# A hybrid RWKV-7 / GLA layer on one core: the second direction's heads in exchanged halves of the array, weight products two groups at a time, and eight tiles moved to a later stage

## The chip, the core and the metric

The kernel is one program on 1 core of a Trainium2 chip. The metric is the device time of one launch in microseconds (us): the median of 3 runs was 1365.04 us (1364.23 to 1368.11).

Engines are named as the profile names them: PE (TensorE, PEld are its weight loads), DVE (VectorE), ACT (ScalarE), POOL (GpSimd) and SP, which issues the DMAs.

## The reference, cut to what matters

256 context tokens and 256 latent tokens of width 2048 go through one layer. A modulated RMSNorm gives `h`; one wide product gives the columns of everything else:

```python
p = h @ lp["w_in"]
(rkv, z_a, lora_w, lora_a, q_b, k_b, v_b, z_b, lora_g, g_a, g_b) = jnp.split(p, _split_points(), axis=-1)
```

An RWKV-7 branch (16 heads of 64) and a GLA branch (4 heads) scan the tokens in both directions, context first; only the latent tokens give output:

```python
y_a = (y_a + bonus.reshape(bsz, t, A_WIDTH)) * jax.nn.silu(f["z_a"])
ob = o_b * lax.rsqrt(jnp.mean(o_b * o_b, axis=-1, keepdims=True) + EPS) * lp["b_norm_g"]
y_b = ob.reshape(bsz, t, B_WIDTH) * jax.nn.silu(f["z_b"])
mixed = (jax.nn.sigmoid(f["g_a"]) * (y_a.astype(dt) @ lp["w_a"])
         + jax.nn.sigmoid(f["g_b"]) * (y_b.astype(dt) @ lp["w_b"]))
return mixed @ lp["w_out"]
```

A gated residual and a last RMSNorm follow. RWKV's per-head step is `S <- S diag(w) + (S a) b^T + v k^T`, `y = S r`.

## The kernel before

**Weight products.** Every weight tile (512 KB) is loaded from HBM as `raw`, split in ACT and DVE into a high part `wH` (a copy) and a low part `wL` (the rest), and multiplied in three matmuls: high by high, low by high, high by low. Such a group of three is the unit in which the order below speaks; on the page it is `acc<-lH,wH`, `acc<-lL,wH`, `acc<-lH,wL` (latent tokens alone, 256 columns) or `acc<-hH,...` (both streams, 512 columns); `pv` and `pout` are the same in other shapes. One tile of 128 columns of `w_in` takes 16 groups. A queue of jobs (`add_cm` and others) says in which order the tiles come; a job can carry a condition (`take`) and be passed over while that fails (`skip`).

**Who sets the order.** The code does not write instructions down in program order. Each piece of work is a generator (a track: `gla_track`, `sc_track`, `inv_track`, ...) that yields operations, bank claims or conditions. `Issue.run` keeps its own clocks of the five engines, built on a table of costs, and emits, step by step, the track that can start first; tracks that start within 40 ns of each other go by priority, and weight products have the last priority, 99: they fill where nothing else is ready. Two rules let a weight product go ahead of ready work: when 1.2 us of other work has gone since the last one (`since`), and when PE's clock threatens to fall by the table (`cooling`). What is emitted is a fixed order for each engine: if an operand is late on the chip, PE stands still, whatever is ready behind.

**The stages.** (1) Modulation vectors, RMSNorm and the first products (0 to 130 us of the profile). (2) The GLA stage, 130 to 582 us: the four GLA heads, the key and value tiles of RWKV (convolved, spilled to DRAM), and, two for each head, the eight tiles of `z_b` (`add_zb`, `sz_track` with key `"b"`): a tanh on ACT, a product on DVE, and the tile waits in SBUF until `gla_track` multiplies it with the transposed head (`pT`) and writes it to `yb` in DRAM. (3) The RWKV stage, 582 to 1166 us, for eight pairs of heads, `p` = 0 to 7. Its filler are the weight products of `r` and `z_a` (as slots come free) and of 32 tiles of the gates, `tg`; `pace` lets tile n go when n <= 17 + 32 x (small work done / 230 us), and all of them after the last pair's features (`"C"`). (4) The products with `w_b`, `w_a` (1166 to 1257 us) and `w_out` (to the end).

**A pair in stage 3.** `fe_track` makes features. `ab_track` makes eight chunk matrices for two directions `d` and two heads `hd`: fp32 matmuls 64 by 64 by 64 (`pab`), which read the half `hd` of the rows and write the half `hd` of the columns. `AB` is their masked copy. `inv_track` inverts them: ACT copies into `Lin`, a DVE transpose to `M`, 60 POOL operations (`tm`, `M`), transposes back, the products `pH` and `pZ`, and copies to `Z`. `sc_track` then goes through eight chunks, a chain in which each step needs the one before: `p1` (matmuls, `p` on the page), a copy `R` on ACT, `pU` (matmuls with `Z`), copies to `UV` on ACT and DVE, `pSs` (matmuls), `Sn` on DVE, copies to `UV`, and in the last four chunks products for the output, `pY`. Names for halves are `half(hd)`: partitions 0 to 63 or 64 to 127. An fp32 matmul stands twice in the profile (two passes): four matmuls are x8 there.

Of the kernel before, what the change touches and what calls it, by code (L numbers as in the profile page):

```python
# [76 lines left out]
class Issue:  # L77
# [253 lines left out]
def hybrid_layer(tc, a, out):  # L331
    nc = tc.nc
    es = ExitStack()
    with es:
# [197 lines left out]
        PACE0, WB = 17, 230e3  # L532
# [213 lines left out]
        yb = dp.tile([P, 8, 256], F32, name="yb")  # L746
        kv = [[dp.tile([P, 512], F32, name=f"kv{i}_{j}") for j in range(2)] for i in range(8)]
# [42 lines left out]

        def sz_track(acc, key):

            if key[0] == "b":
                yield S_sz.has()
                S_sz.n -= 1
# [43 lines left out]
        def gla_track(h, gp):  # L839
# [106 lines left out]
            for j in range(2):  # L946
                yield lambda: ("b", 2 * h + j) in szs
                pT = yield Claim("gg", [P, 2, P], "pT", *ons)
                yield [PE.transpose(pT[:, tt, :], ons[tt][:, j * P:j * P + P], ident) for tt in range(2)]
                sz = szs.pop(("b", 2 * h + j))  # L950
                yield DV.scalar_tensor_tensor(sz, pT.rearrange("p a b -> p (a b)"), bnh[:, j:j + 1], sz,
                                              op0=OP.mult, op1=OP.mult)
                rel(pT)
                yield DM.dma_start(yb[:, 2 * h + j, :], sz)
# [213 lines left out]
        def inv_track(p, fp, xp):  # L1168
# [11 lines left out]
            for hd in range(2):  # L1180
                for blk in range(2):
                    r = slice(64 * hd + 32 * blk, 64 * hd + 32 * blk + 32)
                    cc = slice(32 * blk, 32 * blk + 32)
                    yield AC.copy(RW["Lin"][qs[hd]].rearrange("p t u -> p u t")[:, 16 * blk:16 * blk + 16, :],
                                  AB[r, :, :, cc].rearrange("p i d t -> p (i d) t"))
            yield DV.transpose(M.rearrange("p i c -> p (i c)"), Lin.rearrange("p t u -> p (t u)"))
            for hd in range(2):
                yield AC.copy(RW["GMo"][qs[hd]], AB[64 * hd:64 * hd + 32, :, :, 32:64].rearrange("p i d t -> p (i d) t"))
# [21 lines left out]
            pZ = yield Claim("g3", [P, 16, 32], "pZ", GMo, Lin)  # L1210
            for u in range(0, 16, hq):
                yield [PE.matmul(pZ[64 * hd:64 * hd + 32, u + x, :], RW["GMo"][qs[hd], u + x, :], W[qs[hd], 16 + u + x, :],
                                 start=True, stop=True, tile_position=(qs[hd].start, 64 * hd)) for x in range(hq) for hd in range(2)]
            yield lambda: p < 2 or ("sc1", p - 2) in DONE
            for hd in range(2):
                for blk in range(2):
                    r = slice(64 * hd + 32 * blk, 64 * hd + 32 * blk + 32)
                    yield (DV.tensor_copy if hd else AC.copy)(Z[r, :, 32 * blk:32 * blk + 32], W[qs[hd], 16 * blk:16 * blk + 16, :])
                yield (DV.tensor_copy if hd else AC.copy)(Z[64 * hd:64 * hd + 32, :, 32:64], pZ[64 * hd:64 * hd + 32])
            rel(pZ)  # L1220
# [35 lines left out]
        def sc_track(p, xp):  # L1256
# [8 lines left out]
            for i in range(8):  # L1265
# [6 lines left out]
                b = [PE.matmul(p1[half(hd), d, :], GM[kr, hd, i, d, :], UV[kr, i, d, hd, :], start=True, stop=True)  # L1272
# [187 lines left out]
        def add_zb(i):  # L1460
            add_cm(w_in, C_ZB + P * i, "l", CTX, 12, lambda acc: sz_track(acc, ("b", i)))

# [50 lines left out]
        def pace(n):  # L1513
            return lambda: "C" in DONE or n <= PACE0 + 32 * (iss.small - state.get("b0", iss.small)) / WB

        for n in range(32):
            add_cm(w_in, (C_GA, C_GB)[n % 2] + P * (n // 2), "l", CTX, 12, lambda acc, n=n: tg_track(acc, n // 2, n % 2),
                   take=pace(n), skip=True)
# [132 lines left out]
        state["b0"] = iss.small  # L1651
        iss.groups["acc"] = (0, 1)
# [159 lines left out]
```

## Time and profile before

| what | value |
|---|---|
| median of 3 runs | 1365.04 us |
| the profiled execution's own time | 1361.36 us |
| its span, first to last instruction | 1359.6 us |
| mean granted clock of TensorE | 0.977 |
| busy share of the span: PE, DVE, ACT, POOL | 93%, 71%, 53%, 40% |
| PE matmuls in the trace | 11479 |

Matmuls are pipelined, and the profile models their ends, so a busy PE is not one at its peak. What one kind of work costs PE is read from the distance between starts in the timeline, not from the durations. The granted clock is 1.00 at 2.4 GHz and 0.50 at 1.2 GHz; a mean between them is a mix.

### The profile page before, as it was taken

The numbers are of one execution on the slowest core, as the hardware profiler recorded it, in microseconds if no ns is written. First come the engines' busy times: TensorE is split into PE (matmuls) and PEld (weight loads), VectorE is DVE, ScalarE is ACT, GpSimd is POOL, SyncE is SP. The second block draws the span as 40 slices with busy tenths as digits, with TensorE's granted clock in tenths as the row PEclk, the third lists the DMA queues.
The fourth block names the chain that finished last, engine by engine and source line by source line (L and its number), as shares of the span: only waits on it lengthen the run. The fifth ranks groups of instructions, "written<-read, shape, count | busy, mean of one in ns | idle before, by whom it ended". The sixth has DMA issues, their size and how long they took to land. (4 is left out here: it accounts for less than half of the span.)

```text
span 1359.6 us, 29662 instructions
## 1 busy us (share of the span) xinstructions
PE 1270.1 (93%) x11479; PEld 1068.1 (79%) x11479; DVE 968.3 (71%) x2031; ACT 718.2 (53%) x1449; POOL 543.3 (40%) x684
## 2 busy tenths in 40 slices
PE   5999999999999999999899999799989999999996
PEld 3555578688788897998777778677878888999876
DVE  4433497885965737767978998698978776668656
ACT  5222244343334444486577678667766666445443
POOL 0000476676570000005888729673983550000012
PEclk9999999999999999999889999799979999999999
DMA  9999465455462433576632443234433545789564
GB/s 347 354 340 311 132 195 168 150 171 160 145 202 79 134 102 97 153 196 171 157 85 76 113 118 92 77 99 114 108 78 94 138 105 145 203 247 271 185 230 144
DMA packets 311186, 220.45 MB, mean 162 GB/s; under 512 B 37354, under 2 KB 286724, under 8 KB 310532
## 3 DMA queue, kind: packets, MB, share of 16 engines
q1 hardware_dynamic: 311044, 218.55, 55.5%
q8 instruction: 90, 1.47, 0.4%
q14 instruction: 52, 0.43, 0.1%
HBM read 199.76 MB, written 12.46 MB: 156 GB/s over the span
## 5 line engine op out<-in xcount | busy, mean ns | idle before, releaser
L304 DVE TENSOR_TENSOR wL<-raw,wH 128x512 fp32r<-128x512 f32 x484 | 377.2, 786 | 170.2 <-ACT wH L304 165.0
L304 ACT CAST wH<-raw 128x512 fp32r<-128x512 f32 x484 | 295.1, 616 | 328.5 <-PE acc L304 208.7
L304 PE MATMUL acc<-lH,wH 128*128 128x256 f32 x896 | 285.1, 318 | 0.5 <-ACT tg L304 0.5
L304 PE MATMUL acc<-lL,wH 128*128 128x256 f32 x896 | 256.0, 286 | 0.0
L304 PE MATMUL acc<-lH,wL 128*128 128x256 f32 x896 | 255.6, 285 | 0.2 <-DVE wL L304 0.2
L304 PEld LDWEIGHTS acc<-lH,wH 128*128 128x128 f32 x896 | 173.4, 194 | 21.1 <-issue 4.5
L304 POOL TENSOR_TENSOR tm<-M 64x30 f32<-64x30 f32 (+14 forms) x240 | 160.1, 667 | 74.3 <-DVE M L304 48.1
L304 POOL TENSOR_TENSOR M<-M,tm 64x30 f32<-64x30 f32 (+14 forms) x240 | 170.1, 709 | 18.7
L304 PEld LDWEIGHTS acc<-lL,wH 128*128 128x128 f32 x896 | 174.5, 195 | 3.1 <-issue 1.7
L304 PEld LDWEIGHTS acc<-lH,wL 128*128 128x128 f32 x896 | 173.9, 194 | 0.4 <-DVE wL L304 0.4
L304 PE MATMUL acc<-hH,wH 128*128 128x512 f32 (+1 forms) x416 | 168.7, 406 | 1.3 <-ACT lo L304 1.3
L304 PE MATMUL acc<-hH,wL 128*128 128x512 f32 (+1 forms) x416 | 157.2, 378 | 0.0
L304 PE MATMUL acc<-hL,wH 128*128 128x512 f32 (+1 forms) x416 | 156.3, 376 | 0.1
L304 PEld LDWEIGHTS acc<-hH,wH 128*128 128x128 f32 x416 | 78.6, 189 | 38.1 <-issue 22.9
L304 POOL TENSOR_TENSOR xs<-yg,fg 128x512 f32<-128x512 f32 (+1 forms) x10 | 13.5, 1371 | 231.4 <-DVE yg L304 231.4
L304 POOL TENSOR_TENSOR gw<-gw,csl 128x512 f32<-128x512 f32 x60 | 71.1, 1185 | 61.9 <-DMA gw<-in_w_mod_dram 61.9
L304 PEld LDWEIGHTS acc<-hH,wL 128*128 128x128 f32 x416 | 78.4, 188 | 15.5 <-DVE wL L304 0.4
L304 POOL TENSOR_TENSOR ga<-ga,gw 128x512 f32<-128x512 f32 x60 | 88.6, 1476 | 4.2
L304 PEld LDWEIGHTS acc<-hL,wH 128*128 128x128 f32 x416 | 78.9, 190 | 10.6 <-DVE hL L304 0.4
L304 PE MATMUL acc<-yH,wH 128*128 128x256 f32 x256 | 73.0, 285 | 0.0
L304 PE MATMUL acc<-yL,wH 128*128 128x256 f32 x256 | 72.8, 284 | 0.0
L304 PE MATMUL acc<-yH,wL 128*128 128x256 f32 x256 | 72.8, 284 | 0.0
(318 smaller groups left out, 2627.7 us busy)
## 6 DMA issues: line engine op xcount, KB each, us to landing
raw<-in_w_in_dram SPq DMA_DIRECT2D x174, 512.0 KB, 4.0
wm<-in_w_mod_dram SPq DMA_DIRECT2D x64, 512.0 KB, 6.9
gw<-in_w_mod_dram SPq DMA_DIRECT2D x64, 256.0 KB, 4.0
raw<-in_w_out_dram SPq DMA_DIRECT2D x32, 512.0 KB, 4.8
raw<-in_w_b_dram SPq DMA_DIRECT2D x16, 512.0 KB, 4.1
raw<-in_w_a_dram SPq DMA_DIRECT2D x16, 512.0 KB, 4.9
kv<-kvo SPq DMA_DIRECT2D x16, 256.0 KB, 3.9
tg<-tg SPq DMA_DIRECT2D x32, 128.0 KB, 3.8
```

Of the source, the lines that this page charges most:

```text
L304: op = Op("dma" if name == "dma_start" else self.key, name, lambda: f(*a, **k), aps[0], aps[1:], func, k.get("accum_out"), any(x.tensor.na ...
```

## The change

It has four parts. (a) In `ab_track`, `inv_track` and `sc_track` the second direction's heads (`d` = 1) go to exchanged halves, `half(hd ^ d)`, and the results of the two directions to banks of their own: the four matmuls of `pab` and of `pU` use all four pairs of row half and column half, where before two of them used the same pair. The copies around them are cut by direction: two copies to `UV` after `pU` become four of half the size, four into `Lin` eight, and so for `GMo` and `Z`. (b) `Issue.run` counts the weight products since the last other PE work (`dense`); in stage 3, while that is under 500 ns by its table, the next group follows if it can start within 60 ns, though other work is ready. (c) The eight `z_b` tiles leave stage 2 and become the first of the paced filler jobs of stage 3 (`zs_track`: as before, but spilled to DRAM); `gla_track` only scales its head (on ACT), and `y_track` loads the tiles back and multiplies. (d) The pace is 25 + 40 x (small work done / 230 us), the 32 gate tiles counted from 8.

```diff
+        self.dense = self.run_min = 0.0
...
+                if tr[6] == "pe" and best[0] != 99 and 0 < self.dense < self.run_min:
+                    best = next((x for w, x in c if x[0] == 99 and isinstance(x[3], list)
+                                 and w <= max(w0, self.t["pe"]) + 60), best)
                 if tr[6] == "pe" and best[0] != 99 and 0.6 and self.cooling():
...
                 if best[0] == 99:
                     self.since = 0.0
+                    self.dense += self.work - w0
                 else:
+                    if best[6] == "pe":
+                        self.dense = 0.0
...
-        PACE0, WB = 17, 230e3
+        PACE0, NPACE, WB = 25, 40, 230e3
...
+        zs = [dp.tile([P, 256], F32, name=f"zs{i}") for i in range(8)]
...
+        def zs_track(acc, i):
+
+            yield S_tg.has()
+            S_tg.n -= 1
+            sz = pools["com"].tile([P, 256], F32, name="zs", tag="tg", bufs=2)
+            yield AC.activation(sz, acc, AF.Tanh, scale=0.5)
+            yield DV.scalar_tensor_tensor(sz, sz, 1.0, acc, op0=OP.add, op1=OP.mult)
+            rel(acc)
+            yield DM.dma_start(zs[i], sz)
+            S_tg.n += 1
+            DONE.add(("zs", i))
...
-                yield lambda: ("b", 2 * h + j) in szs
+                yield S_sz.has()
+                S_sz.n -= 1
...
-                sz = szs.pop(("b", 2 * h + j))
-                yield DV.scalar_tensor_tensor(sz, pT.rearrange("p a b -> p (a b)"), bnh[:, j:j + 1], sz,
-                                              op0=OP.mult, op1=OP.mult)
+                ob = pools["com"].tile([P, 256], F32, name="ob", tag="sz", bufs=2)
+                yield AC.activation(ob, pT.rearrange("p a b -> p (a b)"), AF.Copy, scale=bnh[:, j:j + 1])
...
+            pas = []
+            for d in range(2):
+                pas.append((yield Claim("g3", [P, 8, 64], f"pab{d}", *bks, ar)))
             for g in range(2):
-                pa = yield Claim("g3", [P, 4, 2, 64], "pab", *bks, ar)
-                yield [PE.matmul(pa[half(hd), i, d, :], bks[d][half(hd), chunk(4 * g + i, d), xb, :], ar[half(hd), d, i, g, :],
-                                 start=True, stop=True) for i in range(4) for d in range(2) for hd in range(2)]
-                yield DV.tensor_tensor(AB[:, 4 * g:4 * g + 4], pa, RW["m_t"][:, None, None, :].to_broadcast([P, 4, 2, 64]), op=OP.mult)
-                rel(pa)
+                yield [PE.matmul(pas[d][half(hd ^ d), 4 * g + i, :], bks[d][half(hd), chunk(4 * g + i, d), xb, :],
+                                 ar[half(hd), d, i, g, :], start=True, stop=True)
+                       for i in range(4) for d in range(2) for hd in range(2)]
+            for d in range(2):
+                yield DV.tensor_tensor(AB[:, :, d, :], pas[d], RW["m_t"][:, None, :].to_broadcast([P, 8, 64]), op=OP.mult)
+                rel(pas[d])
...
-                for blk in range(2):
-                    r = slice(64 * hd + 32 * blk, 64 * hd + 32 * blk + 32)
-                    cc = slice(32 * blk, 32 * blk + 32)
-                    yield AC.copy(RW["Lin"][qs[hd]].rearrange("p t u -> p u t")[:, 16 * blk:16 * blk + 16, :],
-                                  AB[r, :, :, cc].rearrange("p i d t -> p (i d) t"))
+                for d in range(2):
+                    for blk in range(2):
+                        r = slice(64 * (hd ^ d) + 32 * blk, 64 * (hd ^ d) + 32 * blk + 32)
+                        cc = slice(32 * blk, 32 * blk + 32)
+                        yield AC.copy(RW["Lin"][qs[hd]].rearrange("p t u -> p u t")[:, 16 * blk + 8 * d:16 * blk + 8 * d + 8, :],
+                                      AB[r, :, d, cc])
...
-                b = [PE.matmul(p1[half(hd), d, :], GM[kr, hd, i, d, :], UV[kr, i, d, hd, :], start=True, stop=True)
+                b = [PE.matmul(p1[half(hd ^ d), d, :], GM[kr, hd, i, d, :], UV[kr, i, d, hd, :], start=True, stop=True)
...
-                for hd in range(2):
-                    pU[hd] = yield Claim(("st", "u1")[hd], [P, 2, 64], f"pU{hd}", R)
-                yield [PE.matmul(pU[hd][half(hd), d, :], Z[half(hd), 2 * i + d, :], R[half(hd), d, :], start=True, stop=True)
+                for d in range(2):
+                    pU[d] = yield Claim(("st", "u1")[d], [P, 64], f"pU{d}", R)
+                yield [PE.matmul(pU[d][half(hd)], Z[half(hd ^ d), 8 * d + i, :], R[half(hd ^ d), d, :], start=True, stop=True)
                        for d, hd in DH]
-                yield [(DV.tensor_copy if hd else AC.copy)(UV[us, i, :, hd, :], pU[hd][half(hd)]) for hd in range(2)]
+                yield [(DV.tensor_copy if d else AC.copy)(UV[us, i, d, hd, :], pU[d][half(hd)]) for d, hd in DH]
...
-            add_zb(2 * h)
-            add_zb(2 * h + 1)
...
-            return lambda: "C" in DONE or n <= PACE0 + 32 * (iss.small - state.get("b0", iss.small)) / WB
+            return lambda: "C" in DONE or n <= PACE0 + NPACE * (iss.small - state.get("b0", iss.small)) / WB
...
+        for n in range(8):
+            add_cm(w_in, C_ZB + P * n, "l", CTX, 12, lambda acc, n=n: zs_track(acc, n), take=pace(n), skip=True)
...
+        iss.run_min = 500.0
...
+                yield lambda: ("zs", k) in DONE and ("zs", k + 1) in DONE
+                z = mg["mB"][:, k:k + 2, :]
+                for x in range(2):
+                    yield DM.dma_start(z[:, x, :], zs[k + x])
+                yield DV.tensor_tensor(land[:, k:k + 2, :], land[:, k:k + 2, :], z, op=OP.mult)
                 yield from y_split(1, k, 2, land[:, k:k + 2, :])
```

Three places of the order that comes out of it. The first is on PE in the scan of the first pair, where it takes in the `pab` of the third pair (rows of before):

```order
L304 MATMUL pSs<-UV,BK_6077 64x64 x4
L304 MATMUL pY<-UV,GMr_6079 64x64 x4
L304 MATMUL pab<-ar,bk 64x64 x16
L304 MATMUL acc<-lH,wH 128x256
L304 MATMUL acc<-lL,wH 128x256
L304 MATMUL acc<-lH,wL 128x256
L304 MATMUL p_8097<-UV,GM_6075 64x64 x4
L304 MATMUL pY<-UV,rq 64x64 x4
L304 MATMUL pab<-ar,bk 64x64 x16
L304 MATMUL acc<-lH,wH 128x256
```

The same place of the change (the first half of `pab`, and what follows it):

```order
L311 MATMUL pab_7589<-ar,bk 64x64 x2
L311 MATMUL pab_7590<-ar,bk 64x64 x2
L311 MATMUL acc<-lH,wH 128x256
L311 MATMUL acc<-lL,wH 128x256
L311 MATMUL acc<-lH,wL 128x256
L311 MATMUL acc<-lH,wH 128x256
L311 MATMUL acc<-lL,wH 128x256
L311 MATMUL acc<-lH,wL 128x256
L311 MATMUL p_7631<-UV,GM_5414 64x64 x4
L311 MATMUL pY<-UV,rq 64x64 x4
L311 MATMUL pab_7589<-ar,bk 64x64 x2
```

The 16 matmuls of a half of `pab` now alternate between two banks, two by two, and the weight products between two other pieces of work are two groups, where one stood.

The second place is on ACT, in a step of the scan; before:

```order
L304 COPY R<-p_8097 128x128
L304 CAST wH<-raw 128x512
L304 COPY UV<-pU_8142 64x2x64
```

and of the change:

```order
L311 COPY R<-p_8161 128x128
L311 ACTIVATE ta<-pal,a0h 128x512
L311 COPY UV<-pU_8192 64x64 x2
```

One copy of 128 columns has become two of 64; DVE has the same with the other bank.

The third is on PE at the end of the first GLA head (`pT` are the transposes of its two halves); before, with products of `z_b` around them:

```order
L304 MATMUL acc<-hL,wH 128x256
L304 MATMUL acc<-hH,wL 128x256
L304 MATMUL pT<-ident,on 128x128 x2
L304 MATMUL acc<-hH,wH 128x256
L304 MATMUL acc<-hL,wH 128x256
```

and of the change, with products of 512 columns (key and value tiles) in their place:

```order
L311 MATMUL acc<-hL,wH 128x512
L311 MATMUL acc<-hH,wL 128x512
L311 MATMUL pT<-ident,on 128x128 x2
L311 MATMUL acc<-hH,wH 128x512
L311 MATMUL acc<-hL,wH 128x512
L311 MATMUL acc<-hH,wL 128x512
L311 MATMUL pT<-ident,on 128x128 x2
```

Counted over the whole order of PE, matmuls named `acc`, each once (`pv` and `pout`, 768 and 480, stay where they were): before the first `pq` of stage 3, 1896 before and 1443 in the change; from there to the last `pyt` of stage 3, 2061 and 2430; after it, 747 and 831. The stretches of `acc` in stage 3, from one other piece of work to the next, are 261 before and 241 in the change; before stage 3 they are 147 and 143. PE has 8982 matmuls in both. DVE's splits `wL` are as many as before.

## Rows read from the trace of the kernel before

**Rows 1.** Busy time by stage; columns PE, PEld, DVE, ACT, POOL, granted clock, DMA.

```profile
130.00:582.00 452.00, 436.44 (x2832) 367.45 (x2825) 315.28 (x640) 182.64 (x356) 177.22 (x145) 1.00 0.51 148
582.00:1072.00 490.00, 448.22 (x5490) 389.10 (x5490) 405.01 (x830) 347.10 (x703) 317.66 (x466) 0.94 0.43 111
1072.00:1166.00 94.00, 92.25 (x1118) 80.44 (x1117) 66.11 (x166) 55.98 (x146) 32.07 (x47) 1.00 0.51 138
1166.00:1257.00 91.00, 91.00 (x770) 90.76 (x769) 66.17 (x130) 44.29 (x81) 0.00 (x0) 1.00 0.87 254
1257.00:1360.00 103.00, 90.01 (x480) 76.64 (x478) 62.05 (x102) 44.08 (x86) 13.54 (x10) 0.97 0.56 185
```

**Rows 2.** What PE waited for, 582 to 1072 us: total, times, longest.

```profile
PE pH L304 <- DVE Lin L304: 9.6, 4, 6.9
PE p L304 <- DVE UV L304: 5.3, 11, 1.9
PE pSs L304 <- DVE UV L304: 3.7, 8, 1.0
```

**Rows 3.** PE's timeline around one `pU` of the scan: start, duration.

```profile
700.37 0.28 PE L304 MATMUL acc<-lL,wH 128*128 128x256 f32 x1
700.49 0.28 PE L304 MATMUL acc<-lH,wL 128*128 128x256 f32 x1
700.70 0.45 PE L304 MATMUL pU<-R,Z 64*64 64x64 f32 x8
701.08 0.39 PE L304 MATMUL acc<-lH,wH 128*128 128x256 f32 x1
701.30 0.28 PE L304 MATMUL acc<-lL,wH 128*128 128x256 f32 x1
701.42 0.28 PE L304 MATMUL acc<-lH,wL 128*128 128x256 f32 x1
```

**Rows 4.** PE's timeline at 716 to 722 us, small products next to each other.

```profile
717.01 0.45 PE L304 MATMUL pY<-UV,rq 64*64 64x64 f32 x8
717.39 0.66 PE L304 MATMUL pbt<-ident,bk 128*128 128x128 f32 x4
...
719.62 0.45 PE L304 MATMUL pSs<-UV,BK 128*64 128x64 f32 x8
719.90 0.40 PE L304 MATMUL pY<-UV,GMr 128*64 128x64 f32 x8
720.24 1.15 PE L304 MATMUL pab<-ar,bk 64*64 64x64 f32 x32
721.32 0.39 PE L304 MATMUL acc<-lH,wH 128*128 128x256 f32 x1
```

**Rows 5.** PE's timeline at 24 us: `pg` writes four quarters of the columns.

```profile
24.20 1.50 PE L304 MATMUL pg<-wm,cs 128*32 128x256 f32 x24 [0.28 <-DVE modv L304]
25.64 0.66 PE L304 MATMUL xpt<-ident,xt 128*128 128x128 f32 x4
```

**Rows 6.** Groups of DVE and ACT, 582 to 1166 us: busy us, mean ns | idle before.

```profile
L304 DVE TENSOR_TENSOR wL<-raw,wH 128x512 fp32r<-128x512 f32 x179 | 136.5, 766 | 20.0 <-ACT wH L304 18.9
L304 DVE COPY UV<-pU 64x128 f32<-64x128 f32 x64 | 18.8, 293 | 18.2 <-PE pU L304 14.8 <-ACT UV L304 1.8
L304 DVE TENSOR_SCALAR Sn<-pSs,Dt 128x64 f32<-128x64 f32 x16 | 3.8, 274 | 0.1
...
L304 ACT COPY Lin<-AB 32x512 f32<-32x512 f32 x32 | 34.8, 1088 | 19.0 <-DVE AB L304 18.6
L304 ACT COPY UV<-pU 64x128 f32<-64x128 f32 x64 | 16.4, 256 | 22.5 <-PE pU L304 22.0
```

**Rows 7.** What PE waited for, 130 to 582 us: the first row.

```profile
PE pT L304 <- DVE on L304: 4.2, 2, 2.5
```

**Rows 8.** Busy time of two stretches of 20 us; columns as in rows 1.

```profile
840.00:860.00 20.00, 12.53 (x212) 10.80 (x213) 14.07 (x29) 6.59 (x18) 17.85 (x28) 0.89 0.30 81
860.00:880.00 20.00, 18.20 (x225) 15.59 (x219) 15.05 (x35) 17.15 (x26) 10.67 (x20) 0.77 0.18 44
```

More of the change, by code (lines that the diff above doesn't have):

```diff
@@ L789, in rc_track @@
             rcs[p] = o
+        def zs_track(acc, i):
[8 more added lines that the diff above has]
+            DONE.add(("zs", i))
         def sz_track(acc, key):
-            if key[0] == "b":
-                yield S_sz.has()
-                S_sz.n -= 1
             sz = pools["com"].tile([P, 256], F32, name="sz", tag="sz", bufs=2)
@@ L946, in gla_track @@
             for j in range(2):
-                yield lambda: ("b", 2 * h + j) in szs
+                yield S_sz.has()
+                S_sz.n -= 1
                 pT = yield Claim("gg", [P, 2, P], "pT", *ons)
                 yield [PE.transpose(pT[:, tt, :], ons[tt][:, j * P:j * P + P], ident) for tt in range(2)]
-                sz = szs.pop(("b", 2 * h + j))
-                yield DV.scalar_tensor_tensor(sz, pT.rearrange("p a b -> p (a b)"), bnh[:, j:j + 1], sz,
-                                              op0=OP.mult, op1=OP.mult)
+                ob = pools["com"].tile([P, 256], F32, name="ob", tag="sz", bufs=2)
+                yield AC.activation(ob, pT.rearrange("p a b -> p (a b)"), AF.Copy, scale=bnh[:, j:j + 1])
                 rel(pT)
-                yield DM.dma_start(yb[:, 2 * h + j, :], sz)
+                yield DM.dma_start(yb[:, 2 * h + j, :], ob)
                 S_sz.n += 1
@@ L1180, in inv_track @@
             for hd in range(2):
-                for blk in range(2):
-                    r = slice(64 * hd + 32 * blk, 64 * hd + 32 * blk + 32)
-                    cc = slice(32 * blk, 32 * blk + 32)
-                    yield AC.copy(RW["Lin"][qs[hd]].rearrange("p t u -> p u t")[:, 16 * blk:16 * blk + 16, :],
-                                  AB[r, :, :, cc].rearrange("p i d t -> p (i d) t"))
+                for d in range(2):
[4 more added lines that the diff above has]
+                                      AB[r, :, d, cc])
             yield DV.transpose(M.rearrange("p i c -> p (i c)"), Lin.rearrange("p t u -> p (t u)"))
             for hd in range(2):
-                yield AC.copy(RW["GMo"][qs[hd]], AB[64 * hd:64 * hd + 32, :, :, 32:64].rearrange("p i d t -> p (i d) t"))
+                for d in range(2):
+                    yield AC.copy(RW["GMo"][qs[hd], 8 * d:8 * d + 8, :], AB[64 * (hd ^ d):64 * (hd ^ d) + 32, :, d, 32:64])
             DONE.add(("lin", p))
@@ L1209, in inv_track @@
             yield DV.transpose(W[hs].rearrange("p u i -> p i u"), M)
-            pZ = yield Claim("g3", [P, 16, 32], "pZ", GMo, Lin)
+            pZ = []
+            for d in range(2):
+                pZ.append((yield Claim("g3", [P, 8, 32], f"pZ{d}", GMo, Lin)))
             for u in range(0, 16, hq):
-                yield [PE.matmul(pZ[64 * hd:64 * hd + 32, u + x, :], RW["GMo"][qs[hd], u + x, :], W[qs[hd], 16 + u + x, :],
-                                 start=True, stop=True, tile_position=(qs[hd].start, 64 * hd)) for x in range(hq) for hd in range(2)]
+                yield [PE.matmul(pZ[u // 8][64 * (hd ^ u // 8):64 * (hd ^ u // 8) + 32, u % 8 + x, :], RW["GMo"][qs[hd], u + x, :],
+                                 W[qs[hd], 16 + u + x, :], start=True, stop=True,
+                                 tile_position=(qs[hd].start, 64 * (hd ^ u // 8))) for x in range(hq) for hd in range(2)]
             yield lambda: p < 2 or ("sc1", p - 2) in DONE
             for hd in range(2):
[L1216 to L1220, printed above, removed]
+                for d in range(2):
+                    for blk in range(2):
+                        r = slice(64 * (hd ^ d) + 32 * blk, 64 * (hd ^ d) + 32 * blk + 32)
+                        yield (DV.tensor_copy if hd else AC.copy)(Z[r, 8 * d:8 * d + 8, 32 * blk:32 * blk + 32],
+                                                                  W[qs[hd], 16 * blk + 8 * d:16 * blk + 8 * d + 8, :])
+                for d in range(2):
+                    yield (DV.tensor_copy if hd else AC.copy)(Z[64 * hd:64 * hd + 32, 8 * d:8 * d + 8, 32:64],
+                                                              pZ[d][64 * hd:64 * hd + 32])
+            for d in range(2):
+                rel(pZ[d])
             s["Z"] = Z
@@ L1284, in sc_track @@
                 pU = [None, None]
-                for hd in range(2):
-                    pU[hd] = yield Claim(("st", "u1")[hd], [P, 2, 64], f"pU{hd}", R)
-                yield [PE.matmul(pU[hd][half(hd), d, :], Z[half(hd), 2 * i + d, :], R[half(hd), d, :], start=True, stop=True)
+                for d in range(2):
+                    pU[d] = yield Claim(("st", "u1")[d], [P, 64], f"pU{d}", R)
+                yield [PE.matmul(pU[d][half(hd)], Z[half(hd ^ d), 8 * d + i, :], R[half(hd ^ d), d, :], start=True, stop=True)
                        for d, hd in DH]
-                yield [(DV.tensor_copy if hd else AC.copy)(UV[us, i, :, hd, :], pU[hd][half(hd)]) for hd in range(2)]
+                yield [(DV.tensor_copy if d else AC.copy)(UV[us, i, d, hd, :], pU[d][half(hd)]) for d, hd in DH]
                 rel(pU[0])
@@ L1513, in pace @@
         def pace(n):
-            return lambda: "C" in DONE or n <= PACE0 + 32 * (iss.small - state.get("b0", iss.small)) / WB
+            return lambda: "C" in DONE or n <= PACE0 + NPACE * (iss.small - state.get("b0", iss.small)) / WB
+        for n in range(8):
+            add_cm(w_in, C_ZB + P * n, "l", CTX, 12, lambda acc, n=n: zs_track(acc, n), take=pace(n), skip=True)
         for n in range(32):
             add_cm(w_in, (C_GA, C_GB)[n % 2] + P * (n // 2), "l", CTX, 12, lambda acc, n=n: tg_track(acc, n // 2, n % 2),
-                   take=pace(n), skip=True)
+                   take=pace(n + 8), skip=True)
         mg = {}
```

2 lines of the change are left out of this document (removed).

## The prediction

> **What bounds the kernel now.** I read the stage table first [rows 1]. PE is busy 436 of 452 us in the GLA stage, 448 of 490 us in the RWKV stage up to the last features, 92 of 94 us in its last scan and all of the 91 us behind it; DVE, the next engine, reaches 405 of 490 us. So the time is PE's work plus the time in which PE stands or runs at a lower clock. In the RWKV stage it stands 490 - 448 = 42 us, and its mean clock there is 0.94: 0.06 x 490 = 29 us at full speed are lost to the 1.2 GHz level, though not all of that had work waiting. The second view is who is waited for there [rows 2]: the largest wait is `pH` for the DVE transpose behind POOL's 60 operations (9.6 us in 4 waits), then the scan's `p` and `pSs` for the copies to `UV` (5.3 and 3.7 us). These are waits in a fixed order: PE stands in front of one late operand while weight products lie behind it.
>
> The third view, the timeline, prices PE's work [rows 3]. Inside a stretch of weight products the starts are 0.12 us apart (701.30 to 701.42). Around other work it is dearer: from the last of a stretch to the next piece 0.21 us (700.49 to 700.70), from the first of the next stretch to its second 0.22 us (701.08 to 701.30). `pU` between them, eight passes, takes 0.38 us, where `pSs` with other small work right behind takes 0.28 us (719.62 to 719.90) [rows 3, 4]. So a stretch between two small pieces costs 0.09 + 0.10 + 0.10 = 0.29 us beside its matmuls.
>
> **The change, part by part.**
>
> *Weight products are moved, not removed.* By the count of the order 453 leave the stages before the RWKV stage, 369 come into it and 84 behind it. At 0.12 us each [rows 3] that is -54.4, +44.3 and +10.1 us: zero. A gain must come from what PE does or waits for beside them. That the first stage gets shorter by 54 us on the page will therefore mean nothing by itself.
>
> *The four corners.* `pab` takes 32 passes in 1.08 us, 720.24 to 721.32 [rows 4], 0.034 us each. Two of its matmuls read and write different halves, two share; if two run beside each other now and four could, half of that time goes: about 0.5 us for each of 16 groups of `pab`, 8 us. `pU` has four matmuls in eight passes; half of its 8 x 0.034 = 0.27 us is 0.13 us, but its edges stay, so I take 0.11 us, times 64 steps 7 us. Do four run together? Work in four quarters of the columns does: `pg` streams 24 passes of 256 columns in 1.44 us (24.20 to 25.64), 0.06 us each, where a weight product of 256 columns needs 0.12 us though its passes are single [rows 5, 3]. Two products on the same half of the rows do as well: `pY<-UV,rq` reads one half of the partitions alone and needs 0.38 us for eight passes (717.01 to 717.39), as `pU` does with two [rows 4, 3]. So I take -15 us; the ends are 0 and -17. `pZ` keeps its order (eight chunks of one direction, then of the other) and gains nothing.
>
> The Trainium skill ("TensorE: Matmul & The Clock Gate", Part 3, packing small matmuls) says that a weight load overlaps a matmul in flight only when its row group differs. By that rule the third of four matmuls, on the row half of the second, would wait, the corners would be worth nothing and the sum below would lose its 15 us. The row of `pY<-UV,rq` speaks against it for two matmuls; for four no run here shows it yet.
>
> *Two groups at a time.* The stretches in the RWKV stage go from 261 to 241, before it from 147 to 143. 24 fewer at 0.29 us [rows 3, 4] is -7 us; the ends are 0 and -8. That a group goes ahead of ready work costs the scan at most three matmuls, 0.36 us; PE does useful work in it, so its price is only where the scan itself ends the stage: after the last features (94 us with PE busy 92 [rows 1]) it doesn't.
>
> *More and smaller copies.* After `pU` DVE has two copies of 64 columns for one of 128, which took 293 ns; a 64-column operation from PSUM takes 274 ns (`Sn<-pSs,Dt`) [rows 6]. Two cost between 293 (nothing but columns) and 548 ns; I take +0.2 us in each of 64 steps. ACT's copy beside it (256 ns) grows likewise. `Lin` goes from four copies of 1088 ns to eight; at half a copy and a fixed part of 0.1 us that is +0.8 us for each pair, on the way to POOL. Weight products cover this: a filler stretch stands between `pU` and `pSs` in nearly every step. Where the order's table sees less than the chip takes, PE stands: I put +5 us, between 0 and 64 x 0.25 = +16.
>
> *The tiles of `z_b`.* Their 8 x 16 groups are in the sum above. Their splits, 32 of 766 ns on DVE [rows 6] and as many on ACT, go from the GLA stage to the RWKV stage: there DVE gets some 24 us more on 405 + 66. The 8 writes and 8 reads of 128 KB on SP's queue, behind the loads of `raw`, and 4 products on DVE lie before the first use of `yH` by the `w_b` products, which now start 21 groups after the last scan; hidden by these. Without that cover it would be one load and one product, some 5 us once. In the GLA stage `pT` already waited 4.2 us for DVE with products of `z_b` in front [rows 7]; the products of 512 columns in their place are fewer. I put +4 us for four heads, between 0 and +12.
>
> *Standing and clock in the RWKV stage.* Of the 42 us standing and 29 us of clock [rows 1], 71 in all, some is filled: PE gets 369 more weight products among the same other work, and the lower clock comes behind standing: in 840 to 860 us PE is busy 12.5 of 20 us, in the next 20 us the clock is 0.77 [rows 8]. But the largest wait comes from an order that expects POOL sooner than it is done [rows 2], and that stays. I take a fifth of the standing, 8 us, and a sixth of the clock, 5 us: -13; the ends are -45 (two thirds of it) and +25 (0.4 us in each of 64 steps more).
>
> The sum: 0 - 15 - 7 + 5 + 4 - 13 = **-26 us** on the profiled execution's 1361.4 us: 1335.4. The median of the runs stands 3.7 us above that execution (1365.0), so I forecast 1339 for the median. What the measurement can tell from no change is about 0.3%, 4 us.
>
> **The rivals.**
>
> *Two corners at a time, as before* (the change doesn't do on the array what it says). For it: nothing in the trace shows four of these products together, and only two of them do so now. Against it: [rows 4, 5]. The corner term goes: 1339 + 15 = 1354. The rule of the Trainium skill that is named above would give this time too.
>
> *The filler does more than I think.* For it: 20% more weight products between the same scans, and standing and lower clock come in the same stretch [rows 1]. If two thirds of the 71 us go, 47, that is 34 us more than I took: 1305.
>
> *The GLA stage doesn't shrink by its share.* Without `z_b` its heads' own chain through DVE shows: `pT` waited already [rows 7]. At 5 us more for each of four heads, 20 us are lost: 1359.
>
> *DVE becomes the bound of the scan* (the other side). DVE is busy 471 of 584 us in the RWKV stage [rows 1]; it gets 24 us of splits and 13 us of copies, 508. Its queue is served in order, and a split of 766 ns in front of `Sn` or of a copy to `UV` makes PE stand, as in [rows 2], but in each step. At 0.6 us for each of 64 steps that is +38 us in place of -13: 1361.4 - 26 + 51 + 3.7 = 1390. It decides from 0.2 us more in each step: -26 + 13 + 0.2 x 64 is 0, and what comes above that makes the kernel slower.
>
> **How the numbers follow.** My forecast 0.50, the better filler 0.16, two corners 0.14, the GLA stage 0.08, DVE 0.12. Within my forecast the copies, the GLA stage and the standing move the sum by some 18 us to each side, 1321 to 1357. The range reaches down to half of the better filler, 1316, and up to 1362, past the cases of two corners and of the GLA stage; outside are DVE's case and half of the filler's, 2 in 10. Faster by over 0.3%, below 1361: 0.48 + 0.16 + 0.12 + 0.05 = 0.81. Within 0.3%: 0.02 + 0.02 + 0.02 + 0.01 = 0.07. Slower: 0.12.
>
> **What would show it.** Corners: the 32 passes of a `pab`, now in one piece, in 0.55 us instead of two pieces of 1.08, and `pU` to the next start in 0.27 us instead of 0.38. Stretches: weight products in sixes in the timeline. The stages: the RWKV stage starts some 50 us earlier and lasts as long as before or somewhat more, with a granted clock above 0.94 and standing below 42 us; the products of `w_b` start later after the last scan. I am wrong if `pab` still takes 0.034 us a pass, if waits of `p` and `pSs` for `UV` are over 20 us in sum (DVE's case), or if the stage before shows PE standing by 20 us more than its 16.

## The result, and the profile after

The forecast was 1339 us. The change takes **1380.22 us** (median of 6 runs, 1375.39 to 1385.36) against 1364.63 us before: a ratio of 1.0119, 95% interval [1.0089, 1.0149], so **slower by 16 us [12, 20]**, outside the range. The profiled execution's span is 1373.6 us (1359.6 before), its mean clock 0.975 (0.977). That is one execution; over all six the mean clock is 0.971, where before's runs beside the kernels further down have 0.974 to 0.977. One execution of `before_window44` below took 1687 us at a mean clock of 0.655 and is left out of its time and ratio.

The stages of after, columns as in [rows 1], with bounds where its own stages begin:

```profile
130.00:530.00 400.00, 385.38 (x2392) 315.86 (x2385) 282.17 (x583) 161.42 (x319) 174.90 (x146) 0.99 0.48 143
530.00:1062.00 532.00, 469.87 (x5798) 410.74 (x5796) 447.27 (x942) 382.86 (x854) 318.85 (x460) 0.96 0.44 114
1062.00:1166.00 104.00, 98.75 (x1166) 87.14 (x1165) 72.84 (x189) 63.13 (x169) 38.42 (x53) 0.98 0.57 158
1166.00:1269.00 103.00, 99.73 (x844) 98.91 (x844) 69.39 (x134) 48.66 (x88) 0.00 (x0) 1.00 0.83 240
```

The GLA stage is 52 us shorter, with less standing than before (400.0 - 385.4 = 14.6 us for 15.6). The `w_b`/`w_a` stage is 12 us longer, 10 of them its 84 more weight products. The loss is in the RWKV stage and its last scan: 490 + 94 us became 532 + 104. That is 52 us more, where 369 more weight products at 0.12 us are 44 and the corners and stretches should have taken 22 off. PE stands there for 532 - 470 = 62 us in the stage instead of 42, and for 5 in the last scan instead of 2.

What the change does on the array is what was forecast. PE's timeline of after, one `pab` and one `pU`:

```profile
674.28 0.69 PE L311 MATMUL pab<-ar,bk 64*64 64x64 f32 x32
674.90 0.39 PE L311 MATMUL acc<-lH,wH 128*128 128x256 f32 x1
...
711.53 0.34 PE L311 MATMUL pU<-R,Z 64*64 64x64 f32 x8
711.80 0.70 PE L311 MATMUL pb<-k,bo 128*128 128x256 f32 x2
...
719.29 0.34 PE L311 MATMUL pU<-R,Z 64*64 64x64 f32 x8
719.57 0.39 PE L311 MATMUL acc<-lH,wH 128*128 128x256 f32 x1
```

The 32 passes of `pab` take 0.62 us instead of 1.08 [rows 4], `pU` takes 0.27 to 0.28 us to the next start instead of 0.38 [rows 3]. In the trace the starts of `pab`'s single passes come in fours, some 20 ns from the first to the last, and 58 ns from one four to the next (107 once); before they came in twos with the same distances. So the four corners run together. The groups of the other engines, 530 to 1166 us of after (as [rows 6]):

```profile
L311 POOL TENSOR_TENSOR tm<-M 64x30 f32<-64x30 f32 (+14 forms) x240 | 163.9, 683 | 112.1 <-DVE M L311 82.4 <-DVE rl_t L311 11.5
L311 DVE TENSOR_TENSOR wL<-raw,wH 128x512 fp32r<-128x512 f32 x209 | 161.4, 779 | 22.0 <-ACT wH L311 20.8
L311 ACT COPY Lin<-AB 32x256 f32<-32x256 f32 x64 | 40.8, 638 | 9.7 <-DVE AB L311 8.8
L311 DVE COPY UV<-pU 64x64 f32<-64x64 f32 x128 | 28.3, 221 | 17.9 <-PE pU L311 14.8
L311 ACT COPY UV<-pU 64x64 f32<-64x64 f32 x128 | 26.4, 206 | 24.2 <-PE pU L311 21.6
```

The same first row of before, 582 to 1166 us:

```profile
L304 POOL TENSOR_TENSOR tm<-M 64x30 f32<-64x30 f32 (+14 forms) x240 | 160.1, 667 | 74.3 <-DVE M L304 48.1 <-DVE rl_i L304 7.9
```

A copy to `UV` of 64 columns takes 221 ns on DVE and 206 on ACT, where 128 columns took 293 and 256 [rows 6]: two cost 0.15 us more. `Lin` goes from 4 x 1088 ns to 8 x 638, 0.75 us more per pair. DVE has 30 `wL` more than in [rows 6]. POOL, whose work is the same, sits idle 38 us longer before it can begin, most of it for DVE; but the stage is 52 us longer, so that POOL must stand longer in it, and this row alone names no cause. What PE waited for, 530 to 1062 us of after:

```profile
PE pH L311 <- DVE Lin L311: 9.9, 6, 5.2
PE p L311 <- DVE UV L311: 6.4, 12, 1.5
PE pbt L311 <- DVE bk L311: 5.3, 2, 4.5
PE pSs L311 <- DVE UV L311: 3.9, 5, 1.4
PE p L311 <- DVE eC L311: 3.4, 4, 1.3
```

Against [rows 2] no wait stands out; many small ones for DVE are added. Summed over all rows of the view, PE's waits for DVE grow from 27.8 us (31 waits) to 44.5 (44), those for ACT from 10.0 to 12.9; with the last scan, those for DVE from 29.2 to 49.4, which is 20 of the 24 us by which standing rises. The chain of work that ended last, on the page of before and on that of after:

```profile
PE 21%; DVE 7%; ACT 4%; DMA 2%; issue 2%; SPq 0%; DVEq 0%; ACTq 0%
```

```profile
PE 48%; DVE 20%; POOL 13%; ACT 6%; DMA 6%; issue 6%; SPq 0%; DVEq 0%; ACTq 0%; POOLq 0%
```

The profile could follow before's chain over little of the span, so the shares don't compare; but in after POOL's `M` and `tm` are on it with 13%.

### The profile page after: what moved, and what is told of

It is laid out like the page before. It is cut to its first block, busy times and chain, and to the rows that moved or that the text cites. A ratio compares the mean times of both kernels' runs of the same rounds, so it can differ in the third digit from the quotient of the medians.

```text
span 1373.6 us, 29914 instructions
## 1 busy us (share of the span) xinstructions
PE 1257.2 (92%) x11479; PEld 1054.0 (77%) x11479; DVE 988.5 (72%) x2115; ACT 744.9 (54%) x1593; POOL 548.5 (40%) x684
## 4 chain that ended last, share of the span: by engine, by line
PE 48%; DVE 20%; POOL 13%; ACT 6%; DMA 6%; issue 6%; SPq 0%; DVEq 0%; ACTq 0%; POOLq 0%
PE acc L311 29%; POOL M L311 7%; PE pv L311 6%; POOL tm L311 6%; DVE wL L311 6%; PE pg L311 3%; DMA raw<-in_w_out_dram 2%; ACT Lin L311 2%; ACT wH L311 2%; PE pS L311 1%; DVE Lin L311 1%; PE pout L311 1%; DMA tgl<-tg 1%; DVE UV L311 1%; DVE kvo L311 1%
## 5 line engine op out<-in xcount | busy, mean ns | idle before, releaser
L311 PE MATMUL acc<-lH,wH 128*128 128x256 f32 x928 | 292.8, 316 | 4.0 <-DVE rc L311 2.3
L311 PE MATMUL acc<-lH,wL 128*128 128x256 f32 x928 | 265.7, 286 | 0.2 <-DVE wL L311 0.2
L311 PE MATMUL acc<-lL,wH 128*128 128x256 f32 x928 | 265.9, 286 | 0.0
L311 PEld LDWEIGHTS acc<-lH,wH 128*128 128x128 f32 x928 | 180.4, 194 | 21.6 <-issue 5.1
L311 PEld LDWEIGHTS acc<-lL,wH 128*128 128x128 f32 x928 | 181.4, 196 | 3.0 <-issue 1.7
L311 PEld LDWEIGHTS acc<-lH,wL 128*128 128x128 f32 x928 | 180.8, 195 | 0.4 <-DVE wL L311 0.4
L311 PE MATMUL acc<-hH,wH 128*128 128x512 f32 (+1 forms) x384 | 161.1, 419 | 1.0 <-ACT lo L311 1.0
L311 PE MATMUL acc<-hH,wL 128*128 128x512 f32 (+1 forms) x384 | 149.2, 389 | 0.0
L311 PE MATMUL acc<-hL,wH 128*128 128x512 f32 (+1 forms) x384 | 148.5, 387 | 0.1
L311 PEld LDWEIGHTS acc<-hH,wL 128*128 128x128 f32 x384 | 73.1, 190 | 15.6 <-DVE wL L311 0.4
L311 PEld LDWEIGHTS acc<-hL,wH 128*128 128x128 f32 x384 | 73.3, 191 | 10.4 <-DVE hL L311 0.4
```

What stands on the lines that cost most here:

```text
L311: op = Op("dma" if name == "dma_start" else self.key, name, lambda: f(*a, **k), aps[0], aps[1:], func, k.get("accum_out"), any(x.tensor.na ...
```

## The experiments

For the stretch from the first `pV` to the last `pyt` (the RWKV stage with its last scan) I divide the profiled execution's time by PE's starts and ends: standing, what the lower clock cost while PE worked (half of the time that it worked at 1.2 GHz), and small work (all but weight products, from start to next start, at full clock). Each row is one execution.

| kernel | length us | standing | lower clock | small work |
|---|---|---|---|---|
| before | 582.8 | 43.5 | 24.2 | 214.7 |
| the change | 635.9 | 67.4 | 23.3 | 203.3 |
| only_corners | 628.2 | 65.4 | 47.6 | 199.3 |
| corners_old_order | 595.0 | 64.8 | 24.7 | 204.6 |
| copies_old_order | 589.1 | 51.4 | 22.8 | 214.7 |
| splits_doubled_old_order | 598.0 | 59.1 | 20.9 | 216.9 |
| pool_doubled_old_order | 595.5 | 56.7 | 26.0 | 212.7 |
| pab_doubled_old_order | 587.2 | 42.5 | 14.7 | 229.6 |
| pu_doubled_old_order | 584.7 | 40.9 | 15.7 | 227.9 |
| act_splits_doubled_old_order | 585.0 | 49.2 | 22.2 | 212.7 |
| less_dve_old_order | 576.8 | 45.2 | 17.2 | 213.8 |
| less_dve_and_z_old_order | 602.6 | 55.9 | 33.4 | 213.6 |

(The change and only_corners have more weight products there; the others have those of before.)

**One part at a time.** The hunks of the diff fall into three parts: the corners with their copies, the rule of two groups, and the `z_b` tiles with the new pace.

*only_corners*: the hunks from `ab_track` to `sc_track` alone.

> The exchanged halves and their smaller copies alone (pab, pU on four corners, the copies to UV, Lin, GMo, Z cut by direction); no rule of two groups, z_b in the GLA stage as before. Theory 1, the smaller copies hold up the scan and what feeds POOL: PE's work falls by 15 us, but its standing in the RWKV stage goes from 42 to over 60 us, about 1368. Theory 2, the rule of two groups is what costs: 1350, standing 42 us or less. Theory 3, the z_b tiles in the RWKV stage are what costs: 1350 as well.

1388.14 us, ratio 1.0176 [1.0139, 1.0213]. The small work fell by 15.4 us, as forecast (-15); but standing rose by 22 us, the clock's loss by 23 (in an execution of 1396.62 us, the slowest of its four).

*only_two_groups*: `run_min`, `dense` and their rule alone.

> The rule of two groups of weight products alone, from the RWKV stage on; everything else as before. Theory 1 (copies): 7 us of dearer starts saved, about 1358, standing about 42 us. Theory 2 (two groups go ahead of ready work, what they delay comes late at POOL and DVE): standing over 60 us, about 1380. Theory 3 (z_b): about 1358.

1372.03 us, 1.0051 [1.0026, 1.0076]. What a stretch costs beside its matmuls fell by 4 us in all (2 in the change), not 7.

*only_zb_later*: `zs`, `zs_track`, `y_track`, `pace`.

> The z_b tiles and the pace alone: eight tiles leave the GLA stage and are filler in the RWKV stage, with the spill and the later product; no exchanged halves, no rule of two groups. Theories 1 and 2: the weight products are moved and not removed, 1364 to 1370 (the cover in the GLA stage costs at most a few us). Theory 3 (the tiles' splits on DVE and ACT make the RWKV stage's standing grow): 1380 or more, standing over 60 us.

1391.73 us, 1.0191 [1.0169, 1.0213]: the dearest part alone, with standing of 56.1 us and a clock loss of 38.6 in the stretch.

*without_two_groups*: corners and `z_b`.

> The change without the rule of two groups: exchanged halves and z_b later. Theory 1 (copies): 1370 or more. Theory 2 (rule of two groups): 1350 to 1355. Theory 3 (z_b): 1370 or more.

1390.07 us, 1.0179 [1.0159, 1.02]. The parts don't add up: +23.5, +7.4 and +27 alone, 16 together. Theories 1 (copies) and 3 (`z_b`) each got a slow run, the first by far more than its 1368; the two groups lie between their theories. Each part also writes a new order.

**What a new order alone costs.** Edits of the table that change no work:

```diff
-                win = 40
+                win = 44
```
```diff
-    LAT = {"pe": 200.0, "act": 135.0, "dve": 135.0, "pool": 135.0, "dma": 920.0}
+    LAT = {"pe": 200.0, "act": 140.0, "dve": 140.0, "pool": 135.0, "dma": 920.0}
```

> The kernel before with one number of the planner changed that means nothing by itself: tracks within 44 ns instead of 40 ns of each other go by priority. Theory B (the order of before is one that happens to lie well on this chip, and other orders of the same table do not): 1375 to 1395 with standing and loss of clock in the RWKV stage 20 to 40 us higher in sum. Theory A: 1360 to 1369, as before.

> The kernel before with the table's latency of ACT and DVE at 140 instead of 135 ns, as neutral as the other. Theory B: 1375 to 1395. Theory A: 1360 to 1369.

> The changed kernel with the table's latency of ACT and DVE at 140 instead of 135 ns. Theory B: anywhere from 1360 to 1395, by another order alone. Theory A: 1375 to 1385, as the change.

The first on before: 1373.49 us, 1.0059 [1.0037, 1.0082]. The second on before: 1371.88, 1.005 [1.0024, 1.0077]; on the change 1395.1, 1.0225 [1.0169, 1.0281]. The two on before lie between theories A and B, the one on the change at the upper end of B's, 15 us above the change itself. So against these two orders before's lies well by 7 or 8 us, and the +7 of the two groups is no more than such a shift. To price anything, the order had to be held.

**In the order of before.** From here on the sequence in which `Issue.run` took the tracks in the RWKV stage was written down from before and played back, so that each engine gets its pieces in before's order.

*corners_old_order*: the whole corner layout. `pZ` stays in one bank, and the two multiplications to `AB` stand where the second one was.

> Exchanged halves, four corners and the smaller copies, but in the order of before: from the RWKV stage on the tracks are taken in the recorded sequence of the kernel before, so that PE's pieces of work stand in exactly the old order; only what the pieces cost differs. Theory A (the layout itself costs: more and smaller copies come late): standing in the RWKV stage over 60 us as in only_corners, 1380 or more. Theory B (the layout is good and only the new order that the table makes of it is bad): PE's other work falls by 15 us, standing stays near 42 us and the clock's loss near 24 us, 1350 to 1358.

1378.35 us, 1.0092 [1.0063, 1.0122]. Theory B falls; theory A has its standing, and its time nearly. PE's small work falls by 10 us, its standing rises by 21, and the clock of the profiled execution is the same; over the seven runs, though, the mean clock is 0.968, against 0.975 of before's 22 beside them. From the first `pV` to the last `pyt`:

```profile
PE p L370 <- DVE UV L370: 9.9, 18, 2.7
PE pH L370 <- DVE Lin L370: 9.4, 4, 7.9
PE pSs L370 <- DVE UV L370: 4.5, 10, 0.9
PE p L370 <- issue: 4.0, 3, 1.8
PE pH L370 <- DVE AB L370: 3.8, 1, 3.8
```

In the same stretch of before these are 6.0 us for `p`, 9.6 for `pH` behind `Lin`, 3.9 for `pSs`, and none for `AB`.

*copies_old_order*: before's layout, its copies cut as the change cuts them; so too for `Lin`, `GMo` and `Z`.

```diff
-yield [(DV.tensor_copy if hd else AC.copy)(UV[us, i, :, hd, :], pU[hd][half(hd)]) for hd in range(2)]
+yield [(DV.tensor_copy if hd else AC.copy)(UV[us, i, d, hd, :], pU[hd][half(hd), d, :]) for d, hd in DH]
```

> The layout, the banks and TensorE's work of before, every engine's pieces in the order of before; only the copies to UV, Lin, GMo and Z are cut in two by direction, as many and as wide as in the change. Theory 'the copies sit on the chain that the RWKV stage waits for': the corners in the old order cost 13 us although TensorE's small work fell by 10 us, so the copies alone cost some 20 us, 1380 to 1388, with standing in the RWKV stage well above 42 us. Rival 'the copies are covered, the loss in the old order comes from something else in the exchanged layout (the later multiplications of AB, the banks)': 0 to +4 us, 1364 to 1369. From the durations alone (64 steps x 0.15 us, seven pairs x 0.75 us for Lin) the middle is +10 to +15.

1369.61 us, 1.0034 [1.0009, 1.0059]: +5 us, not +20, near the rival's 0 to +4. The theory that the copies are the loss falls in its size.

*corners_pab_old_order* and *corners_pu_old_order*: half of the layout each (both leave out the reordering between the halves: the chunk matrices reach `Z` in another order than the scan reads them, so the output isn't the layer's; the work is the same).

> Only the first half of the corner layout (pab, AB, Lin, GMo), in the order of before. TensorE saves 0.5 us in each of 14 groups of pab, 7 us; Lin and GMo have 12 copies for 6, some 1.1 us more per pair on the way to POOL. Theory 'the chain pab, AB, Lin, transpose, POOL, pH sets the stage': slower, +3 to +10 us, more standing at pH. Rival 'the scan's steps set it': the saving shows, -7 to -2 us.

> Only the second half of the corner layout (pZ, Z, p1, pU, UV), in the order of before. TensorE saves 0.1 us in each of 64 steps, 6 us; the copies to UV take 0.15 us more in each step on both engines. Theory 'the scan's steps set the stage': the steps get longer by 0.05 us and more, +3 to +13 us, with waits of p for UV of 9 us as in the whole layout. Rival 'the way to POOL sets it': within 4 us of before. With the run beside it the two halves should add up to the +13 us of the whole layout; if not, they work on each other.

1368.34 us, 1.0041 [1.0022, 1.006], and 1371.7, 1.0057 [1.0034, 1.008]. They add up to the whole. Each takes work from PE (6.9 and 4.6 us) and is slower, so both ways count, the one to POOL and the scan's steps; both rivals fall.

**The price of a microsecond on each engine.** One engine at a time is given more, the rest held:

```diff
 yield DV.tensor_sub(L, r, H)
+if <every fifth of the first 160>: iss.emit(DV.tensor_sub(L, r, H))
```

> Everything of before in its order, and every fifth of the first 160 splits of weights on DVE in the RWKV stage and behind it is computed twice: 32 more subtractions of 770 ns, 25 us of DVE, about what moving the z_b products brings there, without a single weight product more. Theory 'DVE's queue is part of what the RWKV stage waits for': +8 to +25 us, and this is what the z_b move costs. Rival 'the z_b move costs by where its weight products stand, not by its splits': within 4 us of before.

> Everything of before in its order, and five of the 30 products of POOL for each pair are computed twice, some 3.5 us for each of seven pairs in the RWKV stage, 24 us of POOL. Theory 'pH stands behind POOL only now and then, the scan's steps set the stage': +3 to +8 us. Rival 'the way to POOL sets it (pH waits for DVE's transpose behind POOL 9.6 us, the largest wait)': +15 to +24 us.

> Everything of before in its order, and each matmul of pab is issued twice in its place: 32 more passes for each of 16 groups, 16 x 1.1 = 17.5 us more on TensorE, nothing on another engine. Theory 'TensorE is not what the RWKV stage waits for at pab': at most 6 us slower, so that the 7 us that the four corners took off pab could not be worth more than 2 or 3. Rival 'TensorE's work counts in full, the corners' loss is all copies': +14 to +18 us.

> Everything of before in its order, and each matmul of pU is issued twice: eight more passes in each of 64 steps, 64 x 0.27 = 17 us more on TensorE, in the scan's own chain, since the copies to UV wait for the second time. Theory 'the scan's chain through UV is waited for': its price is as high as that of 0.27 us of copies, +8 to +17 us. Rival 'a step has room, since a stretch of weight products stands in it': 0 to +6 us.

> Everything of before in its order, and every fifth of the first 160 first halves of the weight splits is computed twice on ACT: 32 more of 617 ns, 20 us of ACT. The same places as in the run that doubled DVE's halves (25 us of DVE cost 16 us). Theory 'DVE alone is short': at most +5 us. Rival 'every engine in the fixed order is waited for in the same measure': 0.65 of 20, +13 us.

The others do the same to `tm` (`j % 6 == 0`), to the matmuls of `pab` and `pU`, and to `AC.copy(H, r)`.

| engine | added us | time, ratio | us more | per us added |
|---|---|---|---|---|
| DVE, 32 `wL` x 0.77 | 25 | 1380.44, 1.012 [1.0082, 1.0157] | +16 | 0.66 [0.45, 0.87] |
| POOL, 40 `tm` x 0.67 | 27 | 1382.69, 1.0125 [1.0075, 1.0175] | +17 | 0.63 [0.38, 0.89] |
| PE, `pab` | 15 | 1372.07, 1.0046 [1.0018, 1.0074] | +6 | 0.4 [0.2, 0.7] |
| PE, `pU` | 13 | 1370.87, 1.003 [1.0007, 1.0054] | +4 | 0.3 [0.1, 0.6] |
| ACT, 32 `wH` x 0.62 | 20 | 1368.19, 1.0006 [0.9977, 1.0035] | +1 | 0.04 [-0.16, 0.24] |

(PE's added time is the rise of the small work in the first table; the intervals are those of the ratios.) So DVE and POOL are what the RWKV stage waits for, at some two thirds of a microsecond for each; PE, busy 448 of 490 us, at a third, and in the scan's own chain no more than elsewhere; ACT hardly at all. The rivals "full price" for PE and "every engine alike" fall; that PE is cheaper than DVE is likely, but their intervals touch. With DVE lengthened, `pSs`, which waited 3.7 us for `UV` [rows 2], shows it most; 582 to 1090 us of that run:

```profile
PE pSs L359 <- DVE UV L359: 11.5, 14, 1.8
```

With POOL lengthened, `pH` is where it shows; 582 to 1090 us of that run:

```profile
PE pH L359 <- DVE Lin L359: 21.7, 7, 9.7
```

That is 12 of the 13 us by which standing rose there. With `pab` doubled, PE's 15 us more came out as 4 in the stretch: in the profiled execution standing didn't rise and the lower clock cost 9.5 us less. The other runs agree in part. Nine of the ten have a mean clock of 0.980 (the tenth 0.928), with `pU` doubled all ten 0.978, and before's 25 beside them 0.974; and over 96 runs of before a clock higher by 0.01 goes with a time shorter by some 8 us. By that, an estimate, clock hides some 5 of the 15 us with `pab` and some 3 of the 13 with `pU`; what hides the rest stays open.

**The other direction.** Less for DVE, more for ACT:

```diff
-yield DV.tensor_copy(Dt[:, 4 * g:4 * g + 4, d], e4 if d == 0 else e4[:, ::-1])
+yield AC.copy(Dt[:, 4 * g:4 * g + 4, d], e4 if d == 0 else e4[:, ::-1])
...
-yield DV.tensor_scalar(tw, tw, 1.0, None, op0=OP.add)
+yield AC.activation(tw, tw, AF.Copy, bias=1.0)
```

> Everything of before in its order, but the copies to Dt (32 of 0.24 us) and the addition of 1 to tw (16 of 0.50 us) are done by ACT instead of DVE: DVE gets 15.8 us less, ACT some 17 us more. Theory 'DVE is waited for, ACT isn't' with the prices of the doubled runs (0.65 for a microsecond of DVE, under 0.1 for one of ACT): -6 to -11 us, 1354 to 1359, with less standing than 42 us in the RWKV stage. Rival 'what an engine costs when it gets more, it doesn't give back when it gets less': -2 to +2 us.

**1358.68 us, 0.9947 [0.9933, 0.9961]: faster than both kernels**, by 7 us for before's 15 us on DVE. In its groups, 582 to 1090 us:

```profile
L359 ACT ACTIVATE tw<-tw 128x512 f32<-128x512 f32 x16 | 10.1, 630 | 0.2
...
L359 ACT COPY Dt<-eC 128x4 f32<-128x4 f32 x32 | 4.7, 190 | 0.0
```

ACT got 15 us and nobody waited for it. The expected fall of standing did not come (45.2 us in the stretch for 43.5); the profiled execution gains its 6 us by a clock loss of 17 us for 24. (Over its five runs the mean clock is 0.980, over before's eleven 0.977.) That a microsecond moved from DVE to ACT is worth 0.5 here is shown; whether it arrives as less standing or as a higher clock is not.

> As the run beside it, and the second head's copies to Z go to ACT too: for seven pairs two copies of 0.71 us and one of 0.69 us leave DVE, 14.7 us, and ACT gets two of 1.09 us and one of 0.58 us, 19 us, behind its own three. Theory 'prices alone count': another -5 to -9 us. Rival 'it counts who waits': Z is read by the scan of its pair and its tiles come free with it, three copies later by 2.8 us on ACT take back what DVE gives, -3 to +3 us beside the other run.

(`(DV.tensor_copy if hd else AC.copy)(Z[...])` becomes `AC.copy(Z[...])`.) 1382.24 us, 1.0117 [1.0092, 1.0142]: 24 us slower than the run beside it, worse than its rival said. What PE waited for, 590 to 1193 us:

```profile
PE pH L359 <- DVE Lin L359: 13.1, 5, 6.9
PE pU L359 <- ACT R L359: 8.1, 4, 3.0
PE p L359 <- DVE UV L359: 4.5, 9, 1.9
PE pq L359 <- ACT Z L359: 3.5, 1, 3.5
```

`pU` waited 0.5 us for `R` before. ACT's timeline shows why it waits 8.1 now; the matmuls `p` for this `R` had started at 750.15:

```profile
750.90 2.16 ACT L359 COPY Z<-Lin 32x512 f32<-32x512 f32 x2
753.07 0.58 ACT L359 COPY Z<-pZ 32x512 f32<-32x512 f32 x1
753.67 0.27 ACT L359 COPY R<-p 128x128 f32<-128x128 f32 x1
```

The moved copies stand in ACT's queue in front of `R`, which the scan needs next; here `pU` starts 2.1 of the 8.1 us late. Of the 26 us by which the stretch is longer than in the run beside it, 11 are standing and 16 are clock (first table). A mean price for an engine doesn't hold for a long block in front of a chain's own operation.

## Why the prediction was wrong

- **Where it failed: "standing and clock in the RWKV stage", -13 us.** It took PE for the bound (busy 448 of 490 us) and the standing for room that more weight products fill. In the profiled execution standing went up by 24 us in the RWKV stage and its last scan, by 27 in all. PE's queue is a fixed order: a weight product fills a wait only where it stands in front of the late operand, and the late operands come from DVE and POOL, which the change gives more work (`z_b`'s splits, the copies) or leaves as they are. The runs with one engine lengthened show this in the order of before, and in the change PE's waits for DVE make 20 of the 24 us; the clock, of which I expected 5 us, gave 1 in the profiled execution.
- **The corners, -15 us.** The work fell as said (-15.4 alone, -11.4 in the change); its worth didn't follow. I priced a microsecond of PE at 1; one more of it measures 0.3 to 0.4, and what one less is worth no run measures alone.
- **The tiles of `z_b`.** "DVE gets some 24 us more on 405 + 66" stood in the text, but no term of the sum took it up, and no reason was given for that; only the rival on DVE counted it. At the measured price of DVE those 25 us alone are +16. That was the largest single omission; the time lay in the rows, its price didn't.
- **More and smaller copies, +5 us.** Measured +5 [1, 8] in the order of before: right, by durations of +0.15 us for a step and +0.75 us for a pair (+0.2 and +0.8 forecast).
- **Two groups at a time, -7 us.** -2 to -4: mis-sized.
- **GLA stage, +4 us; weight products moved, zero.** Near: 14.6 us of standing, 1 less than before, and 52 us shorter for the 54 moved; the rival of a GLA stage that doesn't shrink is out.
- **The rivals.** *Two corners at a time* is out (0.62 us), and so is the Trainium skill's rule ("TensorE: Matmul & The Clock Gate", Part 3) as I applied it: the third of four matmuls does not wait, its passes start within some 20 ns of the first's. *DVE becomes the bound of the scan* (1390 us) had the sign and the engine, not the place: `p` and `pSs` waited 6.4 and 3.9 us for `UV`, under the 20 us I set as its sign. DVE's delay shows spread over many waits.

By the measured prices: +16 (`z_b`'s splits), +5 (copies), 11.4 x 0.35 = -4 (corners) and -2 (stretches) make +15, and +16 was measured. I don't call that proved: with the intervals of the prices the sum is anywhere from some +2 to +26, the order is another one, and an order alone moves 7 us or more. That the two agree to 1 us is luck. Two things stay open. The corners in the order of before cost 13 us, of which the prices explain 5 - 4 = 1; the multiplications to `AB` that stand later there can be 4 (`pH` waits 3.8 us for `AB`), some of the rest may be the lower clock of its runs, and what is left has no name. And `z_b` alone costs 27 us, of which some 16 are splits; its new order, its writes and loads and the two tile buffers that it shares with the gates no run separates.

## What to carry to other kernels

Busy share doesn't say which engine a stage waits for. Lengthen one engine at a time in a held order and read the price of a microsecond; here PE at 91% busy was worth about a third, ACT at 71% next to nothing, POOL at 65% and DVE at 83% about two thirds. Work taken off an engine is worth such a price, not its duration (7 us for 15 taken off DVE), and cover for moved work has to be found on the dear engines too. Where a planner writes the order, compare an edit only after you know what a neutral shift of the order costs.

## What the runs showed of the hardware

Four fp32 matmuls of 64 by 64 on the four corners run together even though two of them share each half of the rows: 0.019 us a pass (0.62 us for 32) against 0.034 with two. And halving a copy saves little on DVE and ACT: 64 columns instead of 128 take 221 for 293 ns and 206 for 256 ns, 256 instead of 512 from SBUF 638 for 1088 ns.
